# A gate product whose weights are split by two transfers instead of by VectorE, in every second step of six blocks

## The chip, the cores and the metric

The kernel runs on one core of one Trainium2 chip. A core has five engines, each with an in-order queue of its own: TensorE (PE, whose weight loads are listed as PEld), VectorE (DVE), ScalarE (ACT), GpSimd (POOL) and SyncE (SP), and 16 DMA engines that all queues share. The metric is the device time of one execution in microseconds; smaller is better. Three runs of the kernel before took 1992.51, 1992.51 and 1994.0 us, so the median is 1992.51.

## The reference

The reference is one layer of a bidirectional encoder for 256 tokens of width 4096, all in float32: a normalised input projection, two groups of attention heads, an output projection added to the residual, and then a gated embedding and a final normalisation. The part that matters here is the last:

```python
ple = jnp.einsum('bsc,cd->bsd', p[i], w_ple[i])
gate = jax.nn.sigmoid(jnp.einsum('bsd,de->bse', rms_norm(x, g_ple[i]), w_ple_gate[i]))
x = x + ple * gate
return rms_norm(x, g_final)
```

The gate product multiplies 256 x 4096 activations by a 4096 x 4096 weight matrix, w_ple_gate.

## The kernel before

**How products are made.** TensorE multiplies values of a reduced float32 format (fp32r in the profile). To keep the accuracy of float32, each operand is kept as two such values, hi and lo, whose sum is the original. The function `mm` (lines 123 to 128) issues three products for each pair of operands: hi by hi (L126), hi by the lo of the weights (L127), lo by the hi of the weights (L128).

**Steps.** All large products are cut into chunks of up to 512 output columns, and each chunk into steps. A step takes two blocks of 128 rows of the weights, 128 x 2 x 512 values or 512 KB, for two tiles of 128 tokens: 2 x 2 x 3 = 12 products. The list `steps` holds all of them in the order in which TensorE runs them, one list written out by hand for the whole kernel.

**How weights arrive.** `fetch` (L825) loads a step's weights on SP's queue into one of four buffers called raw. `convert` (L837) splits them with `split` (L108 and L109): ScalarE rounds raw to hi, then VectorE subtracts, lo = raw - hi. The tiles hi and lo have three buffers each. In the main loop (L886) step i calls `convert` for step i + 2 and `fetch` for step i + 4, and then issues its products. A buffer is overwritten once its last reader has ended; the framework puts in those waits.

**The last phase.** It goes over nine blocks of output columns: blocks 0 to 6 have 512 columns, 7 and 8 have 256. For blocks 0 to 7 the chunk of the gate (16 steps in a block of 512) takes in a small chunk, the product with w_ple (one step), after its first six steps; a block of 512 thus has 17 steps. At the end of a block `done_g` applies tanh on ScalarE (L699), combines gate, embedding and residual on VectorE (L704, L705), takes square sums on ScalarE (L711), and multiplies by the final gain on GpSimd (L712), each stage one step later. After block 8, `finish` scales the rows and stores them. Slots are memory areas reused under one name: B0 to B3 hold the split embedding inputs, the embedding inputs and the final gain in this phase; B4 to B7 held the second half of the activations of the output projection, which ends before block 0, and are used again in block 8, where the split weights of its first pass stay for the second pass.

**GpSimd's queue** in this phase holds three loads issued early (the embedding inputs and the final gain, L664 and L669) and the products of L712, two for a block.

Of the kernel before, what the change touches and what calls it, by code (L numbers as in the profile page):

```python
# [12 lines left out]
F32R = mybir.dt.float32r  # L13
# [5 lines left out]
P = 128  # L19
# [15 lines left out]


def constants():
    """What depends on the shapes alone: rotary frequencies, distances of tokens, and in how many
    of the dilated patterns a pair of tokens stands."""
    half = ROPE // 2  # L40
    inv = (np.float32(THETA) ** (-np.arange(half, dtype=np.float32) / np.float32(half))).astype(np.float32)
    d = np.abs(np.arange(S)[:, None] - np.arange(S)[None, :])
    n = sum(((d % dil == 0) & (d <= w // 2)).astype(np.float32) for w, dil in PATTERNS)
    dist = np.where(n > 0, d.astype(np.float32), np.float32(FAR)).astype(np.float32)
    both = np.stack([dist, n]).reshape(2, NT, P, S).transpose(2, 0, 1, 3)
    return {
        "c_inv": np.ascontiguousarray(np.broadcast_to(inv, (P, half))),
        "c_dist": np.ascontiguousarray(both, dtype=np.float32),
    }


def pi_parts(n=8, bits=6):
    """2 pi cut into parts of few bits, whose products with small integers are exact."""
    from fractions import Fraction

    digits = "31415926535897932384626433832795028841971693993751"
    rest, out = 2 * Fraction(int(digits), 10 ** (len(digits) - 1)), []
    for _ in range(n):
        e = math.floor(math.log2(rest))
        unit = Fraction(2) ** (e - bits + 1)  # L60
        part = (rest // unit) * unit
        out.append(float(part))
        rest -= part
    return out


class Chunk:
    """A block of up to 512 output columns of a product: src is its block of the weights, lhs(kt)
    the split activations of a block of 128 rows. A step takes per of those blocks, for the tokens
    of the tiles ts. keep: where the split weights stay for a later chunk, or come from."""  # L70

    def __init__(self, src, nk, n, lhs, banks, done, needs=lambda j: (), per=2, ts=(0, 1), keep=None):
        self.src, self.nk, self.n, self.lhs, self.banks = src, nk, n, lhs, banks
# [5 lines left out]
def encoder_layer(ctx: ExitStack, tc: tile.TileContext, x, p, positions, g_mix, w_in, g_q_latent, w_uq,  # L79
# [23 lines left out]
        return t.bitcast(F32)  # L103

    def split(hi, lo, src, scale=None):
        """hi + lo = src * scale, each of 12 significant bits."""
        if scale is None:
            nc.scalar.activation(hi, src, AF.Copy)  # L108
            nc.vector.tensor_tensor(lo, src, plain(hi), op=ALU.subtract)  # L109
        else:  # L110
            nc.scalar.activation(hi, src, AF.Copy, scale=scale)
            nc.vector.scalar_tensor_tensor(lo, src, scale, plain(hi), op0=ALU.mult, op1=ALU.subtract)

    def split_rows(hi, lo, src, scale):
        """The same, block by block of rows, each with its own scale."""
        n = src.shape[1]
        for k in range(n):
            nc.scalar.activation(hi[:, k], src[:, k], AF.Copy, scale=scale[:, k:k + 1])  # L118
        for k in range(n):
            nc.vector.scalar_tensor_tensor(lo[:, k], src[:, k], scale[:, k:k + 1], plain(hi[:, k]), op0=ALU.mult,  # L120
                                           op1=ALU.subtract)

    def mm(ps, a, b, start, stop):
        """ps += (a_hi + a_lo)^T (b_hi + b_lo), to float32's accuracy."""
        (ah, al), (bh, bl) = a, b
        nc.tensor.matmul(ps, ah, bh, start=start, stop=False)  # L126
        nc.tensor.matmul(ps, ah, bl, start=False, stop=False)  # L127
        nc.tensor.matmul(ps, al, bh, start=False, stop=stop)  # L128

# [1 line left out]
    ident = cp.tile([P, P], F32, name="ident")  # L131
    gains = slot("T6", [2, P])
    nc.gpsimd.dma_start(gains[:32, 0, :], g_mix[0].rearrange("(k p) -> k p", p=P))
# [62 lines left out]
        nc.scalar.activation(ss[:, :, :half], ss[:, :, half:], AF.Copy, scale=-1.0)  # L196

    def rotate(dst, src, tmp, h):
        """dst = rotary of src, both [P, NT, h, ROPE]; on GpSimd."""
        half = ROPE // 2  # L200
        for t in range(NT):
            c = cc[:, t].unsqueeze(1).to_broadcast([P, h, ROPE])
            s1 = ss[:, t, :half].unsqueeze(1).to_broadcast([P, h, half])
            s2 = ss[:, t, half:].unsqueeze(1).to_broadcast([P, h, half])
            nc.gpsimd.tensor_tensor(dst[:, t], src[:, t], c, op=ALU.mult)
            nc.gpsimd.tensor_tensor(tmp[:, t, :, :half], src[:, t, :, half:], s1, op=ALU.mult)
            nc.gpsimd.tensor_tensor(tmp[:, t, :, half:], src[:, t, :, :half], s2, op=ALU.mult)
        nc.gpsimd.tensor_tensor(dst, dst, tmp, op=ALU.add)
# [1 line left out]
    rs_a, rs_b = stat(NT), stat(NT)  # L210

    def rsqrt_mean(dst, total, n):
        """dst = (total / n + EPS) ** -0.5, by Newton's steps from a guess off the exponent."""
        w = dst.shape[1]
        a, t = rs_a[:, :w], rs_b[:, :w]
        nc.vector.tensor_scalar(a, total, 1.0 / n, EPS, op0=ALU.mult, op1=ALU.add)
        bits = dst.bitcast(I32)
        nc.vector.tensor_scalar(bits, a.bitcast(I32), 1, None, op0=ALU.logical_shift_right)
        nc.vector.tensor_scalar(bits, bits, -1.0, float(0x5F3759DF), op0=ALU.mult, op1=ALU.add)
        for _ in range(3):  # L220
            yield
            nc.vector.scalar_tensor_tensor(t, dst, -0.5, dst, op0=ALU.mult, op1=ALU.mult)
            nc.vector.tensor_tensor(t, t, a, op=ALU.mult)
            nc.vector.scalar_tensor_tensor(dst, t, 1.5, dst, op0=ALU.add, op1=ALU.mult)

# [1 line left out]
    flags, urgent, waiting, running = set(), [], [], []  # L227
    ticks = [0, -9]

# [10 lines left out]
                if next(task, "end") == "end":  # L240
                    pool.remove(task)

# [1 line left out]
    xT = [slot("A_hi", [32, S], F32R), slot("A_lo", [32, S], F32R)]  # L244
    xs, sq = {}, stat(NT * 8).rearrange("p (t c) -> p t c", t=NT)
    junk = cp.tile([P, 512], F32, name="junk")
# [9 lines left out]
            yield  # L256

    def x_turn(b, tps):
        """Row blocks 2b and 2b + 1 of x's transpose."""
        for k in range(2):  # L260
            for t in range(NT):
                c = (2 * (b % 2) + k) * P
                nc.tensor.transpose(tps[k][:, t * P:(t + 1) * P], xs[b // 2][:, t, c:c + P], ident)  # L263

    def x_square(b):
        """A share of x's square sums."""
        i, o = divmod(b, 2)
        if o:
            nc.scalar.activation(xjunk[:, 0], xs[i][:, o], AF.Square, accum_out=sq[:, o, i:i + 1])
        else:  # L270
            nc.vector.scalar_tensor_tensor(xjunk[:, 1], xs[i][:, o], 1.0, xs[i][:, o], op0=ALU.mult, op1=ALU.mult,
                                           accum_out=sq[:, o, i:i + 1])
# [17 lines left out]
    def lhs_x(kt):  # L290
        return xT[0][:, kt], xT[1][:, kt]

    # latents
    c_tok = []
    rq, rqs, rkv = stat(NT), stat(NT), stat(NT)
    cT = {}
# [2 lines left out]
    sums = stat(NT * 6).rearrange("p (c t) -> p c t", t=NT)  # L299

    def turn_c(bs):
        """Pairs of row blocks of the latents' transposes, with their gains."""
        for b in bs:
            tp = bank("tp", [2, S], bufs=2)
            for k in range(2):
# [65 lines left out]
        split(pe[:, 0], pe[:, 1], tp[:, 0])  # L371
        flags.add("kpe")

# [1 line left out]
    ya = [None, None]  # L375
    yb = [None, None]
    E = {}

    def attend(h, q_src, k_src, pe, v, y, dil):
        """One head. q_src(t), k_src(t): [P tokens, 128]; pe: split [64, S] pairs of q and k or None;  # L380
        v(kt): split [P keys, 128]; y: where the result goes, [128, S]."""
        tp = bank("tp", [4, P], bufs=2)
        for t in range(NT):
            nc.tensor.transpose(tp[:, t], q_src(t), ident)  # L384
# [60 lines left out]
    def y_rows(y, h):  # L445
        return y[h // 8][:, h % 8]

    # latent attention: pairs of heads
    pairs = {}

    def done_uq(i):
# [46 lines left out]
        return task  # L498

    class Late:  # L500
        """A slice of a tile that will have been allocated when it is used."""

        def __init__(self, get):
            self.get = get
# [10 lines left out]
    def lhs_c(key):  # L515
        return lambda kt: (cT[key][0][:, kt], cT[key][1][:, kt])

    # gates
    us, yT = {}, {}
    ry = {0: stat(NT), 1: stat(NT)}  # L520

# [50 lines left out]
            flags.add(("yT", dil, c))  # L572
        return task

    # dilated attention: groups of four heads
    grp = {}

    def done_d(i, g):
# [32 lines left out]
            yield  # L611
        return task

# [1 line left out]
    x1 = {}  # L615
    ss1, ss2 = (stat(NT * n).rearrange("p (t c) -> p t c", t=NT) for n in (8, 9))
    x1T = []
# [36 lines left out]
                flags.add("r1")  # L654
        return task

# [1 line left out]
    pT, ple, gF, U = [], {}, [], []  # L658
    part2 = [stat(1) for _ in range(NT)]
    blocks = [(512 * c, 512) for c in range(7)] + [(3584, 256), (3840, 256)]  # L660
# [87 lines left out]
            if t == 0:  # L748
                yield

# [1 line left out]
    M = ("m0", "m1"), ("m2", "m3")  # L752
    turn = [0]

# [45 lines left out]
    for c, (lo, n) in enumerate(blocks):  # L800
# [6 lines left out]

        if c < 8:
            g = gate(done_g(c))
            half = 12 // per  # L810
            add(g, 0, half)
            add(small)
# [9 lines left out]
    raw, halves = {}, {}  # L822
    RAW, AHEAD = 4, 2

    def fetch(i):  # L825
        if i < len(steps):
            ch, j = steps[i]
            if ch.keep and not ch.keep[1]:
                return
            names["raw"] = names.get("raw", 0) + 1  # L830
            raw[i] = wp.tile([P, ch.per, ch.n], F32, tag="raw", name=f"raw{i}", bufs=RAW)
# [5 lines left out]
    def convert(i):  # L837
        if i < len(steps):
            ch, j = steps[i]
            if ch.keep and not ch.keep[1]:  # L840
                halves[i] = ch.keep[0][j]
                return
# [25 lines left out]
    nc.vector.memset(junk, 0.0)  # L868

    def warm_up(n):  # L870
        """Products of zeros, so that the array's clock is up when the data comes."""
        w = bank("m2", [512])
        for _ in range(n):
            nc.tensor.matmul(w, warm[:, :P], warm[:, :512], start=True, stop=True)
# [11 lines left out]
    for i, (ch, j) in enumerate(steps):  # L886
# [9 lines left out]
            x_bank(i + 1)  # L896
        if i == 1:
            x_square(0)
        while converted[0] < lead:
            converted[0] += 1  # L900
            convert(converted[0])
# [48 lines left out]
```

## Time and profile before

| What | Value |
|---|---|
| Median of three runs | 1992.51 us |
| Span of the profiled execution | 1991.1 us |
| Its own time (taken as the median of the runs) | 1992.51 us |
| TensorE busy | 1975.5 us, 99% |
| VectorE busy | 1095.7 us, 55% |
| ScalarE busy | 943.4 us, 47% |
| GpSimd busy | 108.0 us, 5% |
| Bytes moved by DMA | 370.56 MB, 186 GB/s on average |
| Share of the DMA engines in SP's queue | 61.6% |

The profile records one execution. The span goes from the first to the last recorded instruction. A row of a group of instructions names the line of the code, the engine, the operation, the output and the inputs by the program's names, the shapes and the count; then the busy time and the mean of one in ns; then the idle time of the engine just before these instructions, with the engine whose work ended it. Matmuls overlap, so the mean duration of one product is longer than the distance from one to the next. The share of the DMA engines is the mean share of time in which the 16 engines handled packets.

### The profile page before, as it was taken

The page shows a single profiled execution, that of the slowest core. Times are in us where ns is not written, and L with a number is a line of the kernel's source. Part 1 is how long each engine was busy: PE and PEld are TensorE (multiplying, and loading weights), DVE is VectorE, ACT ScalarE, POOL GpSimd, SP SyncE. Part 2 cuts the span into 40 slices and gives each one's busy share as a digit, 9 for nine tenths or more (in the row PEclk, how much of TensorE's full clock was granted, in tenths as well). Part 3 has the DMA queues.
Part 4 walks back from the last instruction along what each step waited for, and adds up shares of the span by engine and source line. Part 5 has one row for each costly group of instructions (what it writes and reads, how often), then busy time and mean ns, then how long its engine had stood idle before and what let it go on. Part 6 is the DMA issues. An engine that isn't in the chain of part 4 may idle for free.

```text
span 1991.1 us, 25012 instructions
## 1 busy us (share of the span) xinstructions
PE 1975.5 (99%) x9549; PEld 1682.4 (84%) x9549; DVE 1095.7 (55%) x1351; ACT 943.4 (47%) x1271; POOL 108.0 (5%) x140
## 2 busy tenths in 40 slices
PE   9999999999999999999999999999999999999997
PEld 8998888888888888888888888888888888888887
DVE  7645556554565645645546555555444455555555
ACT  6544555554444544544535544444444444444443
POOL 1001122110000000000000100000000000000100
PEclk9999999999999999999999999999999999999999
DMA  7666544456666566566665766666666766666665
GB/s 251 189 187 193 167 130 141 142 143 201 187 183 193 162 190 190 159 193 178 172 196 170 227 187 201 211 184 196 187 189 189 236 189 194 196 191 191 189 188 183
DMA packets 200489, 370.56 MB, mean 186 GB/s; under 512 B 11924, under 2 KB 45808, under 8 KB 200112
## 3 DMA queue, kind: packets, MB, share of 16 engines
q1 hardware_dynamic: 198448, 361.80, 61.6%
q0 software_dynamic: 1920, 7.15, 1.0%
q8 instruction: 75, 1.23, 0.3%
q14 instruction: 46, 0.38, 0.1%
HBM read 364.72 MB, written 4.19 MB: 185 GB/s over the span
## 4 chain that ended last, share of the span: by engine, by line
PE 99%; DMA 0%; DVE 0%; SPq 0%; issue 0%; ACT 0%; DVEq 0%; ACTq 0%
PE m L126 31%; PE m L128 31%; PE m L127 31%; PE s L126 1%; PE tp L429 1%; PE s L127 1%; PE s L128 1%; PE o L128 0%; PE o L127 0%; PE o L126 0%; PE tp L384 0%; PE tp L263 0%; PE tp L385 0%; PE tp L558 0%; PE tp L644 0%; DMA T<-in_x_dram 0%
## 5 line engine op out<-in xcount | busy, mean ns | idle before, releaser
L109 DVE TENSOR_TENSOR lo<-raw,hi 128x1024 fp32r<-128x1024 f32 (+3 forms) x693 | 841.4, 1217 | 811.5 <-ACT hi L108 810.9
L108 ACT ACTIVATE hi<-raw 128x1024 fp32r<-128x1024 f32 (+3 forms) x693 | 713.5, 1030 | 847.9 <-PE m L128 752.3
L126 PE MATMUL m<-hi,A_hi 128*128 128x512 f32 (+2 forms) x2072 | 793.9, 383 | 0.0
L127 PE MATMUL m<-lo,A_hi 128*128 128x512 f32 (+2 forms) x2072 | 786.4, 380 | 0.0
L128 PE MATMUL m<-hi,A_lo 128*128 128x512 f32 (+2 forms) x2072 | 786.2, 379 | 0.0
L128 PEld LDWEIGHTS m<-hi,A_lo 128*128 128x128 f32 x2072 | 389.7, 188 | 68.7
L126 PEld LDWEIGHTS m<-hi,A_hi 128*128 128x128 f32 x2072 | 390.0, 188 | 66.3
L127 PEld LDWEIGHTS m<-lo,A_hi 128*128 128x128 f32 x2072 | 390.1, 188 | 65.6
L126 PE MATMUL m<-hi,B 128*128 128x512 f32 (+1 forms) x704 | 271.6, 386 | 0.0
L128 PE MATMUL m<-hi,B 128*128 128x512 f32 (+1 forms) x704 | 267.6, 380 | 0.0
L127 PE MATMUL m<-lo,B 128*128 128x512 f32 (+1 forms) x704 | 267.2, 380 | 0.0
L128 PEld LDWEIGHTS m<-hi,B 128*128 128x128 f32 x704 | 132.1, 188 | 23.0
L127 PEld LDWEIGHTS m<-lo,B 128*128 128x128 f32 x704 | 132.3, 188 | 21.7
L126 PEld LDWEIGHTS m<-hi,B 128*128 128x128 f32 x704 | 132.2, 188 | 21.7
L442 POOL TENSOR_TENSOR acc<-acc,junk 128x256 f32<-128x256 f32 x30 | 29.6, 988 | 779.4 <-ACT junk L440 779.4
L109 DVE TENSOR_TENSOR T<-tp,T 128x512 fp32r<-128x512 f32 (+1 forms) x65 | 44.3, 681 | 30.8 <-ACT T L108 30.4
L712 POOL TENSOR_TENSOR T<-T,B 128x512 f32<-128x512 f32 (+1 forms) x16 | 29.0, 1830 | 349.7 <-ACT Q L711 349.7
L108 ACT ACTIVATE T<-tp 128x512 fp32r<-128x512 f32 (+1 forms) x65 | 38.1, 587 | 0.0
L118 ACT ACTIVATE A_hi<-tp,gT 128x256 fp32r<-128x256 f32 x62 | 25.7, 465 | 8.3 <-PE tp L263 8.3
L406 ACT ACTIVATE T<-s,st 128x256 f32<-128x256 f32 x32 | 14.9, 470 | 30.0 <-DVE st L404 30.0
L422 ACT ACTIVATE T<-T,st 128x256 f32<-128x256 f32 x32 | 14.6, 502 | 29.6 <-DVE st L419 29.6
L120 DVE SCALAR_TENSOR_TENSOR A_lo<-tp,gT,A_hi 128x256 fp32r<-128x256 f32 x62 | 27.0, 477 | 2.4 <-ACT A_hi L118 2.3
(213 smaller groups left out, 947.6 us busy)
## 6 DMA issues: line engine op xcount, KB each, us to landing
raw<-in_w_in_dram SPq DMA_DIRECT2D x320, 512.0 KB, 3.7
raw<-in_w_out_dram SPq DMA_DIRECT2D x128, 512.0 KB, 3.7
raw<-in_w_ple_gate_dram SPq DMA_DIRECT2D x128, 512.0 KB, 3.7
raw<-in_w_in_dram SPq DMA_DIRECT2D x63, 400.0 KB, 3.4
raw<-in_w_uq_dram SPq DMA_DIRECT2D x32, 384.0 KB, 3.3
raw<-in_w_ukv_dram SPq DMA_DIRECT2D x16, 512.0 KB, 3.7
T<-in_x_dram POOLq DMA_DIRECT2D x8, 512.0 KB, 6.0
out_dram<-T SPq DMA_DIRECT2D x16, 256.0 KB, 3.0
```

The lines of the kernel that those rows point to most:

```text
L108: nc.scalar.activation(hi, src, AF.Copy)
L109: nc.vector.tensor_tensor(lo, src, plain(hi), op=ALU.subtract)
L118: nc.scalar.activation(hi[:, k], src[:, k], AF.Copy, scale=scale[:, k:k + 1])
L120: nc.vector.scalar_tensor_tensor(lo[:, k], src[:, k], scale[:, k:k + 1], plain(hi[:, k]), op0=ALU.mult, op1=ALU.subtract)
L126: nc.tensor.matmul(ps, ah, bh, start=start, stop=False)
L127: nc.tensor.matmul(ps, ah, bl, start=False, stop=False)
L128: nc.tensor.matmul(ps, al, bh, start=False, stop=stop)
L406: nc.scalar.activation(e[:, t], s[:, t], AF.Exp, bias=nmax[:, t:t + 1], accum_out=l[:, t:t + 1])
L422: nc.scalar.activation(e[:, t], e[:, t], AF.Copy, scale=rl[:, t:t + 1])
L429: nc.tensor.transpose(tp[:, k, t * P:(t + 1) * P], e[:, t, k * P:(k + 1) * P], ident)
L442: nc.gpsimd.tensor_tensor(acc, acc, sq, op=ALU.add)
L712: nc.gpsimd.tensor_tensor(xc, xc, g_cols(lo, n), op=ALU.mult)
```

## The change

The chunks of the gate in blocks 1 to 6 are marked. In a marked chunk the odd steps (j = 1, 3, ..., 15) are no longer loaded by SP into raw and no longer converted by ScalarE and VectorE. Instead:

- `dma_hi`, called seven steps ahead, takes one of the slots B4 to B7 in turn and issues on GpSimd's queue a load of the weights straight into hi; the destination's format is fp32r, so the transfer rounds.
- `dma_lo`, called four steps ahead, lets ScalarE write lo = -hi, and then issues on GpSimd's queue a second load of the same weights that adds to lo. The result is lo = weights - hi.

The even steps, the embedding's steps and all other blocks are handled as before. The slot of a step is numbered by half its place in the list of steps; since the embedding's step shifts the count by one, the earlier user of a slot lies eight or nine steps back in most cases, and seven steps back for the gate steps at places 8, 10 and 12 of blocks 2, 4 and 6. The rest of the diff takes out comments.

```diff
         if c < 8:
             g = gate(done_g(c))
+            g.dma = 1 <= c <= 6
...
+    def by_dma(i):
+
+        ch, j = steps[i] if i < len(steps) else (None, 0)
+        return ch is not None and getattr(ch, "dma", False) and j % 2 == 1
+
+    def source(i):
+        ch, j = steps[i]
+        w = ch.per * P
+        return ch.src[w * j:w * (j + 1), :].rearrange("(k p) n -> p k n", p=P)
+
+    def dma_hi(i):
+        if by_dma(i):
+            ch, j = steps[i]
+            both = slot(f"B{4 + (i // 2) % 4}", [2, ch.per, ch.n], F32R)
+            halves[i] = both[:, 0], both[:, 1]
+            nc.gpsimd.dma_start(halves[i][0], source(i))
+
+    def dma_lo(i):
+        if by_dma(i):
+            hi, lo = halves[i]
+            nc.scalar.activation(lo, plain(hi), AF.Copy, scale=-1.0)
+            nc.gpsimd.dma_start(lo, source(i), accum_op=ALU.add)
...
-            if ch.keep and not ch.keep[1]:
+            if ch.keep and not ch.keep[1] or by_dma(i):
                 return
...
             ch, j = steps[i]
+            if by_dma(i):
+                return
             if ch.keep and not ch.keep[1]:
...
         if i == 1:
             x_square(0)
+        dma_hi(i + 7)
+        dma_lo(i + 4)
         while converted[0] < lead:
```

## The prediction

> **What bounds the kernel now.** I read the page first: share by engine, the slices, the queues, and the chain of waits.
>
> ```profile
> span 1991.1 us, 25012 instructions
> ...
> PE 1975.5 (99%) x9549; PEld 1682.4 (84%) x9549; DVE 1095.7 (55%) x1351; ACT 943.4 (47%) x1271; POOL 108.0 (5%) x140
> ...
> PEclk9999999999999999999999999999999999999999
> DMA  7666544456666566566665766666666766666665
> ...
> q1 hardware_dynamic: 198448, 361.80, 61.6%
> q0 software_dynamic: 1920, 7.15, 1.0%
> ...
> PE 99%; DMA 0%; DVE 0%; SPq 0%; issue 0%; ACT 0%; DVEq 0%; ACTq 0%
> ```
>
> TensorE is busy 99% of the span and is 99% of the chain that ended last. VectorE, from which the change takes work, is 0% of it. The DMA engines are busy six tenths nearly everywhere. Next the timeline of ScalarE: the tanh that ends a block marks its boundary.
>
> ```profile
> 1651.88 0.69 ACT L699 ACTIVATE Q<-m,st 128x512 f32<-128x512 f32 x1 [0.98 <-PE m L128]
> ...
> 1698.12 0.69 ACT L699 ACTIVATE Q<-m,st 128x512 f32<-128x512 f32 x1 [0.98 <-PE m L128]
> ...
> 1929.32 0.69 ACT L699 ACTIVATE Q<-m,st 128x512 f32<-128x512 f32 x1 [0.98 <-PE m L128]
> ```
>
> From 1651.88 to 1929.32 lie blocks 1 to 6, the six that change: 277.44 us, 46.24 each. A block has 17 steps (16 of the gate, one of the embedding), so a step takes 2.72 us, and with 12 products a step one product takes 226.7 ns. The windows of blocks 1 and 6 (columns: stretch, length, busy time and count of PE, PEld, DVE, ACT, POOL, granted clock, DMA share, GB/s):
>
> ```profile
> 1651.88:1698.12 46.24, 46.24 (x205) 38.30 (x204) 25.34 (x22) 20.64 (x24) 3.87 (x2) 1.00 0.64 194
> 1883.08:1929.32 46.24, 46.24 (x205) 38.30 (x204) 25.35 (x22) 20.64 (x24) 3.88 (x2) 1.00 0.62 189
> ```
>
> In both, PE is busy for the whole window at a granted clock of 1.00, and the blocks have one length to the hundredth. Nothing ahead of TensorE is late: there is no wait here to win back. What can change is that something new comes late, and the DMA columns are where the change puts its load.
>
> **The change, part by part.** In each block the 8 odd gate steps change: 48 steps in all.
>
> *VectorE and ScalarE.* The groups by line, blocks 1 to 6:
>
> ```profile
> L109 DVE TENSOR_TENSOR lo<-raw,hi 128x1024 fp32r<-128x1024 f32 x103 | 138.3, 1352 | 126.5 <-ACT hi L108 126.5
> L108 ACT ACTIVATE hi<-raw 128x1024 fp32r<-128x1024 f32 x102 | 108.1, 1060 | 141.3 <-PE m L128 125.6 <-ACT hi L108 5.7 <-PE tp L128 5.0
> L712 POOL TENSOR_TENSOR T<-T,B 128x512 f32<-128x512 f32 x12 | 23.2, 1956 | 285.6 <-ACT Q L711 285.6
> ```
>
> 48 subtractions of 1.35 us go: 65 us less on VectorE, worth 0, since it idled for 126.5 us behind ScalarE there. 48 roundings of 1.06 us go from ScalarE and 48 negations of the same shape come: 0. The even steps' conversions stay hidden, as they now have the three converted buffers to themselves; with that cover gone, one instruction of each (2.4 us) would lie on the path per even step.
>
> *Queues.* SP loses 48 loads of 512 KB; GpSimd gains 96 issues. GpSimd's own timeline of its DMAs, then the issues by line (last column: median us from issue to landing):
>
> ```profile
> 1116.09 3.63 POOL L629 DMA_DIRECT2D T<-in_x_dram  x5
> ...
> 1577.90 0.56 POOL L669 DMA_DIRECT2D B<-in_g_final_dram  x1 [4.72 <-PE m L128]
> ```
> ```profile
> raw<-in_w_ple_gate_dram SPq DMA_DIRECT2D x128, 512.0 KB, 3.7
> ...
> T<-in_x_dram POOLq DMA_DIRECT2D x8, 512.0 KB, 6.0
> ...
> B<-in_g_final_dram POOLq DMA_DIRECT2D x2, 1024.0 KB, 8.0
> ```
>
> An issue costs GpSimd 0.56 to 0.73 us; two per pair of steps are 1.5 of 5.44 us, and the two products of L712 add 3.9 us once a block: GpSimd has room, 0. It is in order, though: the rounding transfer for step X waits until TensorE has ended the last reader of its slot (step X-8 or X-9; at places 8, 10 and 12 of blocks 2, 4 and 6, where the embedding's step shifts the count, X-7), and the accumulating transfer of X-2 queues behind it. Those who wait for GpSimd are TensorE (for lo, at L127) and, once a block, the final scaling, far off.
>
> *The DMA engines.* Before, a block moved 17 loads of 0.524 MB. After, it moves 9 plain loads, 8 rounding loads and 8 accumulating ones. No row shows an accumulating transfer; it reads its target beside its source, so I count it as two units, the ends being one (the second read is free) and four. With two, a block carries 9 + 8 + 16 = 33 units, 17.3 MB; in 46.24 us that is 374 GB/s. The nearest row is the stretch in which five software loads came beside the plain ones:
>
> ```profile
> 1118.00:1128.00 10.00, 10.00 (x48) 8.31 (x47) 5.35 (x11) 3.67 (x4) 1.72 (x3) 1.00 1.01 387
> ```
>
> The engines were full there and gave 387 GB/s: 17.3 MB take 44.7 us, 97% of a block. By the other price, a share of 0.63 in a step of 2.72 us, a unit is 1.71 us and 33 units 56.4 us, 10.2 more than a block, 61 us over six. Packets stretch at partial load, so I hold the full stretch for nearer: the engines will be full, but not in themselves short. With one unit per accumulating transfer (25 x 1.355 us) a block needs 33.9 us. The rounding is priced like a copy, for lack of a row. None of these ends is a gain, since no transfer is waited for now.
>
> *The new chain of one odd step* is what full engines make late. It has 7 steps, 19.0 us, from the slot's release to use (6 steps, 16.3 us, at the nine places named): rounding transfer, negation (1.06), accumulating transfer. At the light load of the rows above: 6.0 + 1.06 + 8.0 (the 1024 KB load, for two reads) = 15.1 us, which fits. Under the full engines of that stretch the software loads landed as follows (the issues of that stretch, and the spread of the same tile's landings):
>
> ```profile
> T<-in_x_dram POOLq DMA_DIRECT2D x5, 512.0 KB, 6.4
> ```
> ```profile
> DMA to landing us min/median/max: 4.0/6.4/10.2
> ```
>
> The last of the five took 10.2. Two such landings make 10.2 + 1.06 + 10.2 = 21.5 us. It doesn't fit in 7 steps: a step stretches to 21.5 / 7 = 3.07 us, a block to 52.1, 5.9 more, 35 us over six. I take this end, because after the change the load is that of the full stretch (374 against 387 GB/s) throughout. The ends are 0 and the 61 us above. While ScalarE waits for a rounding transfer, the conversion of X-1 and the block's tanh and squares queue behind it; they have over two steps in hand.
>
> The Trainium skill's page Collectives: The Full Stack, in its part on why ReduceScatter is half of AllGather, says that an add within a DMA needs two source reads on one ring and so halves the rate; no run here shows that yet. The Trainium skill's page DMA: Bandwidth & Descriptors (section Anatomy of one DMA) gives a software transfer 2.0 us and bytes over 436 GB/s; by that, an estimate, the two landings are 3.2 and 4.4 us and the whole change is hidden. The trace's unhurried landing of 512 KB, 6.0 us, disagrees with 3.2.
>
> *Sum.* Blocks 1 to 6: 277.4 + 35 us; the head, block 0, blocks 7 and 8 and the tail unchanged. Span 1991.1 + 35 = 2026 us. The profiled execution's time is taken as the median of the runs, 1992.51, 1.4 us over the span: 2027.5 us.
>
> **The rivals.**
>
> *Hidden.* Landings stay at 6 to 8 us, and the chain fits as worked out (15.1 us; 1.2 us to spare at the nine short places, 4.0 elsewhere). For it: a share far from full today, and 33.9 of 46.24 us if the second read is free. Against it: 97% if it isn't. Time 1992.5 (1989 to 1996).
>
> *Short places alone.* Only the nine miss. If each of the two landings is 1.5 us longer, the chain is 18.1 us: under 19.0, but 1.8 over 16.3, nine times, 16 us: 2009. It decides from 1.2 us of extra landing on, and from 4.0 us on it is the forecast.
>
> *A much slower add.* If an accumulating transfer takes four plain ones of 1.71 us, a block needs 17 x 1.71 + 8 x 6.84 = 83.8 us: 226 us in all, 2218. Nothing in the trace speaks against it; at 2.7 plain loads it is 118 us, 2110. The rounding could be such a slow form as well.
>
> *Faster.* The distance between products is 226.7 ns for 512 columns, and 120 ns for 256:
>
> ```profile
> 1976.59 0.28 PE L126 MATMUL m<-hi,A_hi 128*128 128x256 f32 x1
> 1976.71 0.28 PE L127 MATMUL m<-lo,A_hi 128*128 128x256 f32 x1
> ```
>
> So 256 columns cost 106.7 ns, and 13.3 ns stay fixed for each product. If this came from VectorE's traffic in the same memory, the odd steps' half of it would go: 6 x 204 x 13.3 ns / 2 = 8 us, 1984. It decides from a pace of 223 ns down. Against it: block 6 is as long as block 1 and VectorE is busy for only 55% of either, yet the pace shows no second value.
>
> **How the numbers follow.** The forecast (a chain too long under full engines, 20 to 70 us) 0.41; a much slower add or rounding (over 70) 0.20; short places alone (4 to 20) 0.17; hidden 0.18; faster 0.04. A measurement of this kernel tells 0.2% (4 us) from no change. So faster 0.04, same 0.18, slower 0.78. The range starts at 1989, the low end of hidden, and goes up to 2110, the add at 2.7 plain loads; left out are the faster case and the upper part of the slow add, under 2 in 10. The forecast's own range is 2012 to 2063.
>
> **What would show it.** Right: the blocks' tanhs stand about 52 us apart; DMA share over 0.9 in that window; PE idle before L127, ended by the accumulating transfer; VectorE 65 us less busy. Hidden: 46.24 again. Short places alone: only blocks 2, 4 and 6 longer. A slow add: blocks of 60 us and more. Wrong, too, if the wait showed at the even steps' conversions, queued late behind the negation.

## The result, and the profile after

The changed kernel takes 2005.45 us (2004.42 to 2009.53, four runs) against 1992.62 us before on the same chip: a ratio of 1.0067, with a 95% interval from 1.0053 to 1.0082. It is 12.8 us slower. The forecast was 2027.5, 35 us slower: the sign and the range held, the size did not. The profiled execution is the longest of the four, 2009.53 us with a span of 2007.8, so its own loss is some 17 us (16.7 between the spans); sums over its rows are to be held against that.

The page of the changed kernel: busy time, the slices of the DMA engines, the two queues, and the chain that ended last.

```profile
span 2007.8 us, 24976 instructions
...
PE 1982.0 (99%) x9549; PEld 1680.4 (84%) x9549; DVE 1034.2 (52%) x1303; ACT 936.4 (47%) x1271; POOL 194.7 (10%) x236
...
DMA  7666544446656566565565766666566769999985
...
q1 hardware_dynamic: 185392, 336.64, 53.8%
q0 software_dynamic: 28032, 57.49, 12.6%
...
PE 90%; DMA 3%; issue 3%; POOL 2%; DVE 0%; ACT 0%; SPq 0%; POOLq 0%; DVEq 0%; ACTq 0%
```

VectorE is 61.5 us less busy (65 were forecast for the 48 subtractions), and this bought nothing. The slices of blocks 1 to 6 now read 9 where they read 6. The chain, which was all TensorE, has DMA, issues and GpSimd in it. The six blocks, cut at their tanhs (columns as in the prediction: stretch, length, busy time and count by engine, granted clock, DMA share, GB/s):

```profile
1652.44:1699.31 46.87, 46.87 (x208) 38.81 (x207) 14.05 (x13) 19.74 (x24) 16.43 (x16) 1.00 1.10 280
1699.31:1749.86 50.55, 48.08 (x207) 38.05 (x206) 15.83 (x13) 19.50 (x25) 18.21 (x18) 1.00 1.04 259
1749.86:1798.63 48.77, 47.06 (x206) 38.09 (x205) 15.27 (x13) 19.38 (x24) 18.04 (x18) 1.00 1.09 272
1798.63:1848.56 49.93, 48.00 (x208) 38.30 (x207) 15.26 (x13) 19.39 (x24) 18.17 (x18) 1.00 1.07 265
1848.56:1896.94 48.38, 47.13 (x206) 38.05 (x205) 15.24 (x13) 19.40 (x25) 18.06 (x18) 1.00 1.08 271
1896.94:1945.93 48.99, 46.36 (x199) 36.73 (x198) 16.56 (x14) 18.42 (x23) 14.74 (x14) 1.00 1.00 249
```

They take 293.5 us instead of 277.4, and these 16.1 us are nearly the whole loss of 16.7. (A tanh can itself start late behind ScalarE's other work, so the cuts between single blocks are less sharp than the sum.) Blocks 2, 4 and 6, which hold the nine short places, run 4.3, 3.7 and 2.8 us over 46.24; blocks 1, 3 and 5 run 0.6, 2.5 and 2.1 over. Two things can be read here at once. The share sums the time of all packets, so a share over 1 means that packets overlapped on an engine: it isn't a fill level that ends at 1. And the block with the least loss, block 1, moved the most per microsecond (280 GB/s), so the others were not held at a ceiling of GB/s.

Who waits for whom in blocks 1 to 6 (waiting instruction, its releaser, us in total, times, longest), and a part of TensorE's weight loads in block 2 (start, duration, in brackets the idle time and its releaser):

```profile
POOL B L847 <- ACT B L846: 150.2, 41, 6.4
ACT B L846 <- DMA B<-in_w_ple_gate_dram: 112.4, 32, 6.7
...
POOL B L841 <- PE m L128: 28.1, 13, 4.2
...
PEld m L127 <- DMA B<-in_w_ple_gate_dram: 15.3, 17, 2.1
...
PEld m L127 <- DVE lo L109: 3.3, 5, 1.0
```
```profile
1710.74 0.19 PEld L127 LDWEIGHTS m<-lo,A_hi 128*128 128x128 f32 x1 [0.74 <-DVE lo L109]
...
1714.08 0.19 PEld L127 LDWEIGHTS m<-B,A_hi 128*128 128x128 f32 x1 [0.71 <-DMA B<-in_w_ple_gate_dram]
...
1722.89 0.19 PEld L127 LDWEIGHTS m<-B,A_hi 128*128 128x128 f32 x1 [0.76 <-DMA B<-in_w_ple_gate_dram]
...
1729.02 0.19 PEld L127 LDWEIGHTS m<-B,A_hi 128*128 128x128 f32 x1 [0.82 <-DMA B<-in_w_ple_gate_dram]
...
1741.35 0.19 PEld L127 LDWEIGHTS m<-B,A_hi 128*128 128x128 f32 x1 [1.57 <-DMA B<-in_w_ple_gate_dram]
```

TensorE waits at L127, as forecast, 17 times for the accumulating transfer and five times for a subtraction that came late behind the negation on ScalarE: 18.6 us by the weight loads. Counted in steps of 2.72 us, the five rows are places 4, 5, 8, 10 and 14 of block 2. Two of them (8 and 10) are short places; the others are not. Over the six blocks, 6 of the 17 waits for the accumulating transfer, 4.9 of 15.3 us, lie at short places: at places 8 and 10 of blocks 2, 4 and 6, and none at place 12. GpSimd waits 28.1 us for TensorE to free a slot, and 150.2 us for negations, which themselves wait for rounding transfers. The issues of the two lines (median landing of their 96 transfers, then of the 80 plain loads of the same weights that are left), and the spread of each line's landings, first the rounding ones (L841), then the accumulating ones (L847):

```profile
B<-in_w_ple_gate_dram POOLq DMA_DIRECT2D x96, 512.0 KB, 8.5
raw<-in_w_ple_gate_dram SPq DMA_DIRECT2D x80, 512.0 KB, 7.3
```
```profile
DMA to landing us min/median/max: 4.6/9.5/11.9
```
```profile
DMA to landing us min/median/max: 5.9/8.2/11.2
```

### The profile page after: what moved, and what is told of

It reads as the page before. It is cut to its first block, busy times and chain, and to the rows that moved or that the text cites. A ratio compares the mean times of both kernels' runs of the same rounds, so it can differ in the third digit from the quotient of the medians.

```text
span 2007.8 us, 24976 instructions
## 1 busy us (share of the span) xinstructions
PE 1982.0 (99%) x9549; PEld 1680.4 (84%) x9549; DVE 1034.2 (52%) x1303; ACT 936.4 (47%) x1271; POOL 194.7 (10%) x236
## 3 DMA queue, kind: packets, MB, share of 16 engines
q0 software_dynamic: 28032, 57.49, 12.6%
## 4 chain that ended last, share of the span: by engine, by line
PE 90%; DMA 3%; issue 3%; POOL 2%; DVE 0%; ACT 0%; SPq 0%; POOLq 0%; DVEq 0%; ACTq 0%
PE m L127 28%; PE m L126 28%; PE m L128 28%; DMA B<-in_w_ple_gate_dram 3%; PE s L126 1%; POOL B L847 1%; PE tp L429 1%; PE s L127 1%; POOL B L841 1%; PE s L128 1%; PE o L128 0%; PE o L127 0%; PE o L126 0%; PE tp L384 0%; POOL T L712 0%
## 5 line engine op out<-in xcount | busy, mean ns | idle before, releaser
L109 DVE TENSOR_TENSOR lo<-raw,hi 128x1024 fp32r<-128x1024 f32 (+3 forms) x645 | 779.3, 1210 | 889.2 <-ACT hi L108 888.8
L108 ACT ACTIVATE hi<-raw 128x1024 fp32r<-128x1024 f32 (+3 forms) x645 | 660.9, 1027 | 705.6 <-PE m L128 626.3
L126 PE MATMUL m<-hi,A_hi 128*128 128x512 f32 (+2 forms) x1880 | 719.3, 383 | 0.0
L127 PE MATMUL m<-lo,A_hi 128*128 128x512 f32 (+2 forms) x1880 | 712.4, 379 | 1.4 <-DVE lo L109 1.2
L128 PE MATMUL m<-hi,A_lo 128*128 128x512 f32 (+2 forms) x1880 | 711.7, 379 | 0.0
L127 PEld LDWEIGHTS m<-lo,A_hi 128*128 128x128 f32 x1880 | 354.0, 188 | 61.5 <-DVE lo L109 3.7
L128 PEld LDWEIGHTS m<-hi,A_lo 128*128 128x128 f32 x1880 | 353.6, 188 | 61.5 <-DVE A_lo L120 0.2
L127 PE MATMUL m<-lo,B 128*128 128x512 f32 (+1 forms) x704 | 267.2, 380 | 0.0
L127 PEld LDWEIGHTS m<-lo,B 128*128 128x128 f32 x704 | 132.3, 188 | 21.6
L846 ACT ACTIVATE B<-B 128x1024 fp32r<-128x1024 f32 x48 | 50.9, 1060 | 168.3 <-DMA B<-in_w_ple_gate_dram 112.4
L127 PE MATMUL m<-B,A_hi 128*128 128x512 f32 (+1 forms) x232 | 87.9, 379 | 8.8 <-DMA B<-in_w_ple_gate_dram 8.6
L128 PE MATMUL m<-B,A_lo 128*128 128x512 f32 (+1 forms) x232 | 86.2, 371 | 0.0
L126 PE MATMUL m<-B,A_hi 128*128 128x512 f32 (+1 forms) x232 | 86.1, 371 | 0.0
L847 POOL DMA_DIRECT2D B<-in_w_ple_gate_dram x48 | 57.9, 1207 | 199.5 <-ACT B L846 196.7
L127 PEld LDWEIGHTS m<-B,A_hi 128*128 128x128 f32 x232 | 43.7, 188 | 22.3 <-DMA B<-in_w_ple_gate_dram 15.3
```

The source lines that it names most:

```text
L846: nc.scalar.activation(lo, plain(hi), AF.Copy, scale=-1.0)
L847: nc.gpsimd.dma_start(lo, source(i), accum_op=ALU.add)
```

## The experiments

The theories were four: the DMA engines are full and set the length of a block; the chain of transfer, negation and transfer is too long for its window everywhere; only the nine short places are; GpSimd's in-order queue holds transfers back. All runs below are medians of five or more (the three slots: four) and were timed beside the kernel before, which stood at 1992.6 to 1992.8 us.

**Slots in turn.** The slots B4 to B7 go round by a counter instead of by half the step's number, so the nine short places are gone.

```diff
-            both = slot(f"B{4 + (i // 2) % 4}", [2, ch.per, ch.n], F32R)
+            tags = (4, 5, 6, 7)
+            both = slot(f"B{tags[taken_slots[0] % len(tags)]}", [2, ch.per, ch.n], F32R)
+            taken_slots[0] += 1
```

> The four slots are handed out in turn, so that the last reader lies eight or nine steps back everywhere; the nine short places are gone. If the short places cost the time (in the profile of the changed kernel blocks 2, 4 and 6 take 50.6, 49.9 and 49.0 us, blocks 1, 3 and 5 take 46.9, 48.8 and 48.4), the even blocks come down to the odd ones' 48 us and the time falls by about 6 us, to some 2000. If the DMA engines' work itself sets the length of a block, nothing changes: 2005 again, and what one place wins is lost at the next. If it is the length of the chain everywhere, a gain of 2 to 4 us.

Measured: 1996.68 us, ratio 1.0021 (1.0012 to 1.0031). 8.8 of the 12.8 us are gone, more than the six that the difference between even and odd blocks gave. The row of GpSimd's wait for a slot, in blocks 1 to 6, fits this:

```profile
POOL B L844 <- PE m L128: 3.4, 6, 0.9
```

It was 28.1 us. A rounding transfer that waits for its slot holds everything that is queued behind it on GpSimd; that a short place so makes later places late, too, and the odd block after it, is the reading of this row and of the waits at other places, not a test of its own. TensorE's weight loads still wait 6 times for the accumulating transfer, 5.5 us.

**Five slots and more lookahead.** B1 is free in these blocks and becomes a fifth slot, handed out by the same counter.

```diff
+            tags = (4, 5, 6, 7, 1)
...
-        dma_hi(i + 7)
-        dma_lo(i + 4)
+        dma_hi(i + 9)
+        dma_lo(i + 5)
```

> B1 as a fifth slot, the rounding transfer called nine steps ahead and the accumulating one five; the transfers and their bytes are the same. If the chain (rounding transfer, negation, accumulating transfer, some 20 us) is too long for its seven steps, two more steps (5.4 us) hide it: blocks near 46.3 us, 1993 to 1996. If the engines are full in themselves (their share in the changed blocks is 1.00 to 1.10), more lookahead wins nothing beyond the first block: 2003 to 2006.

Measured: 1992.92 us, ratio 1.0001 (0.9992 to 1.0010). The loss is gone, with the same transfers and bytes. Blocks 1 to 6 of this run:

```profile
1652.00:1930.00 278.00, 278.00 (x1228) 230.18 (x1227) 85.90 (x79) 116.25 (x137) 106.02 (x102) 1.00 1.08 279
```

TensorE is busy throughout, with the DMA engines at a share of 1.08 and 279 GB/s, and the tanhs of its blocks stand 46.24 us apart again:

```profile
1653.36 0.69 ACT L699 ACTIVATE Q<-m,st 128x512 f32<-128x512 f32 x1 [3.70 <-PE m L128]
...
1930.80 0.69 ACT L699 ACTIVATE Q<-m,st 128x512 f32<-128x512 f32 x1 [6.42 <-PE m L128]
```

From the first to the last lie 277.44 us, as before the change. The accumulating transfers land even later here (median 10.6 us), and TensorE doesn't wait for them. Engines too full to carry these transfers in time are refuted as the cause of the loss; what was short was time ahead.

**No addition.** The second transfer overwrites lo and no longer adds to it. Lo is then the weights instead of the remainder.

```diff
-            nc.gpsimd.dma_start(lo, source(i), accum_op=ALU.add)
+            nc.gpsimd.dma_start(lo, source(i))
```

> The second transfer overwrites lo and does not add to it (lo is then the weights and not the remainder); order, slots, waits and counts stay. It prices the addition. If the add reads its target at the price of a second load, the landing of the second transfer falls from 8.2 us towards 6 us, the share of the DMA engines in a block falls from 1.05 to about 0.85, and the time falls to 1993 to 1997. If the addition costs nothing beside its write, landing and share stay, and the time stays at 2005.

Measured: 1993.15 us, ratio 1.0003 (0.9993 to 1.0012). The medians of the landings fall from 9.5 to 5.5 us for the rounding transfer and from 8.2 to 5.4 for the second one. Blocks 1 to 6, and its software queue on the page:

```profile
1652.00:1930.00 278.00, 278.00 (x1230) 229.86 (x1230) 90.64 (x79) 117.66 (x138) 80.70 (x102) 1.00 0.90 277
```
```profile
q0 software_dynamic: 28032, 57.49, 9.6%
```

Without the addition the change is hidden, even with the short places and with the products of L712 on GpSimd. It isn't the reading of the target alone, though: the issue on GpSimd is recorded with 0.71 us instead of 1.2, too.

The run prices the addition, if a rounding transfer takes the engines as long here as there. Queue q0 before took 1.0% of 1991.1 us; here it takes 9.6% of 1990.9, so 96 transfers (all rounding ones, since lo is fp32r as well) took 171 us of all 16 engines, 1.78 each. With the additions it takes 12.6% of 2007.8 us (the changed kernel) or 12.0% of 1992.6 (five slots): 1.0 to 1.3 us more per accumulating transfer, 2.8 to 3.1 in all, 1.6 to 1.7 rounding ones. The same sum for the run with every fourth step below (7.2% of 1991.9) gives 3.4, or 1.9. The packet records of the traces need no such difference. In blocks 1 to 6, 94% of the packets of 2048 bytes on q0 last 98 or 99 ns in this run; with the additions just under half of them do, and about as many last 176 or 178 ns. That is 1.8 times a rounding packet; against the packets of SP's plain loads, which last mostly 84 ns (the changed kernel) or 98 ns (five slots), it is 2.1 or 1.8 times. GB/s doesn't show it (277 against 279): the target's bytes aren't counted. The rounding transfer lands after 5.5 us here, the plain software load of the trace before after 6.0, in another stretch and beside another load.

**The gain's products on VectorE.** L712 leaves GpSimd's queue.

```diff
-                    nc.gpsimd.tensor_tensor(xc, xc, g_cols(lo, n), op=ALU.mult)
+                    nc.vector.tensor_tensor(xc, xc, g_cols(lo, n), op=ALU.mult)
```

> The products with the final gain (L712), two for a block, go from GpSimd to VectorE. If they hold up the transfers queued behind them on GpSimd (3.0 to 3.9 us once a block), one late step in each block gets earlier and the time falls by 3 to 6 us, to about 2000. If the engines or the chain set the pace, it stays at 2005. VectorE has room (15 of 49 us busy).

Measured: 2000.62 us, ratio 1.0041 (1.0027 to 1.0056): 4.8 us won with the slots as in the changed kernel, though the two intervals (this one and 1.0053 to 1.0082) just overlap. In the changed kernel's trace the two products, 3 us, stand in front of a rounding transfer that follows without a wait, in block 3:

```profile
1758.56 3.00 POOL L712 TENSOR_TENSOR T<-T,B 128x512 f32<-128x512 f32 x2
1761.02 1.21 POOL L841 DMA_DIRECT2D B<-in_w_ple_gate_dram  x1
```

**Both of these.** Slots in turn and the gain on VectorE.

> Four slots in turn and the products with the gain on VectorE, the two edits that won 8.8 and 4.8 us alone. If the rest of the four slots in turn (3.9 us over the kernel before) is the hold-up by these products on GpSimd, it is hidden now: 1993. If it is the chain or the queue's order at full engines, 1995 to 1997.

Measured: 1993.77 us, ratio 1.0008 (0.9998 to 1.0017). The two edits together hide the change but for at most 0.17%, with four slots and no more lookahead; TensorE is busy for all of blocks 1 to 6 in this trace.

**The fifth slot alone.** Five slots in turn, calls at seven and four.

> Five slots in turn, but the calls at seven and four steps ahead as in the changed kernel, so GpSimd's queue keeps its order: the rounding transfer of X+4 stands behind the accumulating one of X, which waits for X's negation. Against five slots with calls at nine and five (1992.9) and four slots in turn (1996.7). If the wait for slots is what was left there, this run is hidden too: 1993 to 1994. If it is the order on GpSimd's queue (a transfer can't be issued before the negation of the step two before it; landing 9.3, negation 1.1 and issues 1.9 us make 12.3 us against 11.6 us for four steps of 46.24 / 17 x 17 / 16), it stays at 1996 to 1997.

Measured: 1996.84 us, ratio 1.0018 (1.0009 to 1.0028), as with four in turn: slots are not what is left. In blocks 1 to 6 GpSimd still waits for negations, and not once for a slot:

```profile
POOL B L850 <- ACT B L849: 167.4, 45, 7.1
```

**Only the order on GpSimd.** The same with the rounding call at nine, which puts the rounding transfer of X+4 ahead of the accumulating one of X.

```diff
-        dma_hi(i + 7)
+        dma_hi(i + 9)
```

> Five slots in turn and the accumulating call at four steps ahead as in the run with the slots alone (1996.8); only the rounding call goes from seven to nine, which puts the rounding transfer of X+4 ahead of the accumulating one of X on GpSimd's queue, so it no longer waits for X's negation. If that order was what was left, the run is hidden: 1993. If it was the place of the accumulating call (four against five steps, the other edit of the run that hid everything), it stays at 1996 to 1997.

Measured: 1994.39 us, ratio 1.0010 (1.0000 to 1.0020). In blocks 1 to 6 GpSimd's wait for negations falls from 167.4 to 22.5 us, and it waits 130.0 us for slots instead, further ahead:

```profile
POOL B L844 <- PE m L128: 130.0, 37, 6.2
...
POOL B L850 <- ACT B L849: 22.5, 8, 4.5
```

Some 2.4 of the remaining 4.1 us go by this edit: by the order, or by the two steps of lookahead that the rounding transfer gets with it, which the run doesn't part. The run with the accumulating call at five instead of four has the rest, 1.5 us. The intervals of this run overlap with those of both its neighbours, so these two sizes are rough. They also don't add up with those of the products of L712: what four slots in turn leave, 3.9 us, goes either with the products off GpSimd or with five slots and the calls at nine and five.

**Three slots.** The chain tested by size.

```diff
+            tags = (4, 5, 6)
...
-        dma_hi(i + 7)
+        dma_hi(i + 6)
```

> Three slots in turn (calls at six and four, so that the queue's order stays). A test of the chain by size: a slot is taken for the chain and its own step, so a block lasts at least 8/3 of (chain + 2.72 us). With a chain of 18 to 20 us (landings 9.3 and 7.7, negation 1.1, issues), a block takes 55 to 61 us and the time is 2045 to 2080. If slots and chain don't matter but only the engines or the order of the queue, it stays within 10 us of the four slots in turn: 1997 to 2007.

Measured: 2041.43 us, ratio 1.0244 (1.0221 to 1.0267), just under the range expected. A block takes (2041.43 - 1992.71) / 6 + 46.24 = 54.4 us; three slots make eight turns of it, so a turn is 54.4 x 3 / 8 = 20.4 us, and without its own step of 2.72 the chain is 17.7. (The profiled execution, the shortest of the four, has blocks of 53.5 us, which gives 17.3.) The landings of this run, rounding and accumulating:

```profile
DMA to landing us min/median/max: 4.1/5.4/10.7
```
```profile
DMA to landing us min/median/max: 5.7/8.8/12.6
```

5.4 + 1.06 + 8.8 is 15.3 us; the issues (some 0.7 and 1.2 us), where they don't lie within the landings, and waits in the queues are the rest. The count by the ring of slots holds here: with too few of them, the chain sets the length of a block.

**Every fourth step.** Half of the transfers, two slots in turn (`tags = (4, 5)`), so the window stays at seven or eight steps.

```diff
-        return ch is not None and getattr(ch, "dma", False) and j % 2 == 1
+        return ch is not None and getattr(ch, "dma", False) and j % 4 == 1
```

> Only every fourth step (j = 1, 5, 9, 13) is split by transfers, with two slots in turn, so that the last reader still lies eight or nine steps back; the even steps and the other odd ones go the old way. Half the added transfers. If landings are long because the engines are full, they fall from 9.3 and 7.7 us towards the 6.0 and 6 to 8 us of a light load and the chain fits: 1993. If an accumulating or rounding transfer is as slow by itself, landings stay, and the time is some 1994 to 1995, half of the loss that is left with four slots in turn.

Measured: 1993.87 us, ratio 1.0011 (1.0001 to 1.0020), between the two expectations. The landing of the accumulating transfers falls to a median of 5.9 us, that of the rounding ones only from 9.3 to 8.1. With half of the transfers the landings are shorter, then, but this run doesn't part the load of the engines from the waiting within the software queue.

## Why the prediction was right in sign and wrong in size

- *Nothing to win.* Right. VectorE lost 61.5 us of work, and the best variants stand at the kernel before (1992.92 to 1993.77) and not below. The rival that the change makes products faster falls: with TensorE never waiting, blocks take 46.24 us again.
- *The DMA engines, full but not in themselves short.* Right as a verdict: five slots carry every transfer with no loss. The price of two units for an accumulating transfer was near: 2.8 to 3.4 us are 2.1 to 2.5 units of 1.355 us or 1.6 to 2.0 of 1.71, and its packets last 1.8 to 2.1 times a plain one's. The price by share (56.4 us for a block, 61 us in all) is refuted: with five slots a block takes 46.24 us with all its transfers. The 387 GB/s were what the engines gave in one stretch; no run here shows their limit.
- *The chain of one odd step.* This is the step that failed, in two terms. The first is the landing: it took 10.2 us, the last of five software loads issued at once, for both. The medians are 9.5 and 8.2 us, and 9.5 + 1.06 + 8.2 = 18.8 us, not 21.5. In block 2 the time from a slot's release to the end of TensorE's wait was 18.1 us at place 8 and 18.8 at place 10: about what seven steps give (19.0 us), and more than the six of the short places (16.3). The second is the stretch: 21.5 us were spread over seven steps and all 17 steps of a block stretched by it, 5.9 us a block. Counted as in the run with three slots, where a turn of a slot is the chain and the slot's own step, four slots and 21.5 us make two turns of 24.2 us, a block of 48.4 us, 13 us over six. That this comes near the measured 12.8 is luck: with the chain of 17.7 to 18.8 us the same count gives 41 to 43 us, under a block. So the chain didn't stretch all steps; the loss came from the short places and from GpSimd's order.
- *Short places alone*, the rival with 16 us and 2009, chance 0.17, was the nearest case. Evening out the slots wins 8.8 of 12.8 us, so it had the larger part of the cause, and its size was near. It wasn't right in place: 11 of TensorE's 17 waits for an accumulating transfer lie elsewhere.
- *GpSimd has room: 0.* Wrong, and it is the rest of the loss. Its time is free (10% busy), its order is not: taking the products of L712 off it wins 4.8 us with the slots as in the change and hides what is left with the slots in turn, and calling the rounding transfers ahead of the accumulating ones wins some 2.4 us with five slots. The prediction named what is queued behind the waits and then priced it at nothing. An accumulating issue is also recorded with 1.2 us where the trace before had 0.56 to 0.73, but the next issue's record starts 0.75 us after it, so little of that holds up the queue.
- *Conversions late behind the negation*, named as a sign of being wrong: they are there, 3.3 us of waits at the even steps, a sixth of the waits.
- *A much slower add* falls: about two plain transfers, not four. *Hidden* is true with five slots and the calls at nine and five, and nearly so with four slots in turn and the products off GpSimd.
- The Trainium skill's page Collectives: The Full Stack, in its part on why ReduceScatter is half of AllGather, lets the second source read halve the rate; the packets here last 1.8 to 2.1 times a plain one's, near that and far from a free read. The Trainium skill's page DMA: Bandwidth & Descriptors (section Anatomy of one DMA) gives, worked out as an estimate, 3.2 us for a software transfer of 512 KB; the shortest median here is 5.4 us beside the other loads. That the change is hidden, which followed from that estimate, isn't true of the kernel as changed.

What stays open: how much the order on GpSimd and how much the longer lookahead of the rounding transfer wins; how the last 1.5 us divide between the place of the accumulating call and the noise of the runs; and how much of the long landings is load of the engines and how much is order within the software queue.

## What to carry to other kernels

Work taken off an engine that waits anyway bought nothing here, and the transfers that replaced it brought a chain of their own. What decided was not the bandwidth but whether issue, landing, second operation and second landing fitted between the release of a buffer and its next use. Count that window in steps for each buffer, and look for the places where another item in the list makes it one step shorter. An in-order queue with 10% busy time can still be the limit: for each wait on it, price what is queued behind.

## What the runs showed of the hardware

- An accumulating software transfer of 512 KB into the core's memory took 2.8 to 3.4 us of all 16 engines, by the difference of queue shares, against 1.78 for a rounding one without addition. Its packets of 2048 bytes last 176 or 178 ns, those of a rounding transfer 98 or 99, those of a plain load on SP's queue mostly 84 or 98. The bytes of its target don't appear in the counted GB/s (279 against 277).
- Its issue is recorded with 1.2 us on GpSimd, against 0.71 for one without an addition. The next issue's record starts 0.75 us after it all the same, and is then long itself, as in block 2 of the changed kernel:

```profile
1727.12 1.22 POOL L847 DMA_DIRECT2D B<-in_w_ple_gate_dram  x1 [4.68 <-ACT B L846]
1727.87 1.21 POOL L841 DMA_DIRECT2D B<-in_w_ple_gate_dram  x1
```

- The share of the DMA engines can stand at 1.08 over six blocks, with 279 GB/s counted, while no product waits for a transfer (five slots, calls at nine and five).
